# Splitting half of an output projection's weights early, and running dense steps ahead of two phase borders, in a hybrid recurrence and attention kernel

## The chip, the cores and the metric

The kernel runs on one core of one Trainium2 chip. The metric is device time in microseconds for one execution. Three executions of the kernel before took 2696.61, 2696.66 and 2698.05 us; the median is 2696.66 us.

## The reference, cut to what matters

One layer (DEPTH = 1) over 2048 tokens of width 1024, all in float32. The input is normalised and modulated, multiplied by one combined projection, and the columns go to two branches: a gated linear recurrence in both directions (HGRN2, 8 heads of 128) and a 2-D neighbourhood attention over a 32 x 64 grid (16 heads of 64). Both results are gated, joined to 2048 columns, and multiplied by one output projection `w_out` of 2048 x 1024.

```python
mod = c_act @ ada_w[l] + ada_b[l]
shift, scale, gate = jnp.split(mod, 3, axis=-1)
h = (_layernorm(x) * (1.0 + scale[:, None, :]) + shift[:, None, :]).astype(x.dtype)
proj = h @ w_in[l]
q_h, i_h, zf_fw, zf_bw, g_h, q_n, k_n, v_n, g_n = jnp.split(proj, split_pts, axis=-1)
y_hg = _hgrn2_branch(q_h, i_h, zf_fw, zf_bw, g_h, lb_fw_all[l], lb_bw_all[l], hg_norm_g[l])
o_na = _neighbourhood_attention(na_heads(q_n), na_heads(k_n), na_heads(v_n), rpb[l])
...
y_na = o_na * jax.nn.silu(g_n)
y = jnp.concatenate([y_hg, y_na], axis=-1) @ w_out[l]
z = DEEPNORM_ALPHA * x + gate[:, None, :] * y
x = (_layernorm(z) * ln_g[l] + ln_b[l]).astype(x.dtype)
```

## The kernel before, in words

**Products in three passes.** A float32 product is made of three TensorE passes in the format fp32r. Each operand is split into `hi` (a ScalarE copy into fp32r) and `lo` (a VectorE subtraction of `hi`), and the passes are hi x hi, hi x lo and lo x hi. `proj_mm` (L259) does this for the input projection, `y_mm` (L1418 to L1420) for the output projection. The normalised input lies in SBUF as 32 row tiles `h{g}_{k}_{s}` of 128 x 512: two groups `g` of 512 tokens, eight slices `k` of the width, and `s` for hi and lo. They hold one half of the tokens (1024) at a time.

**Phases.** After the start, phase `n0` does the attention of the first rows; phase `h` does the recurrence, 16 units `i` (8 heads for the first half of the tokens, then 8 for the second); phase `n1` does the rest of the attention, 8 units `u` (a pair of heads each); phase `wo` does the output projection and the last normalisation. The first four token tiles (`NE = 4`) have the first half of their output projection (the eight slices `k` = 0 to 7 of `w_out`, which belong to the recurrence's columns, in two halves `n` of 512 output columns) made already in the last unit of `n1`, by `out_stream`.

**Who sets the order.** On TensorE the order is that of the program (`manual_schedule`). The other queues, SP's DMA queue among them, are ordered by a planner that simulates the program and issues what is ready; `pinned(...)` keeps one instruction behind everything traced before it on its engine. All DMAs here are issued by SP.

**Weaving.** In each unit a generator `mix` (the recurrence's chain `hgrn`, or the attention's `natten_woven`) is interleaved by `weave` with a generator `dense` of projection steps for the next unit. `mix` yields the weight of each of its parts; after each, `dense` is advanced to the same share of its total. A recurrence unit has a sum of 54 and 80 dense steps (10 outputs of 8 steps; the constant `KUS = 0.68` is the planned length of a step); an attention unit a sum of 24 and 48 steps.

**The recurrence's chain** (`hgrn`), for each of two groups `g`: `rates` (L411 to L425), `ends` (L431 to L444), transposes `turned` (L450), the states' updates `updates` (L458), whose PSUM tile is read by `forward_states` (L469, L471) before the second updates can write it, the factors of the scores (L482 to L518), scores (L497, L525), masks (`masked`) and `outputs` (L549, L551).

**Entering n1.** The steps in front of the first unit are written out: keys (`st.k`, copies within SBUF by DMA on L923), queries, a bias table (`st.table`, L702, 480 KB each; three buffers), V tiles (`st.v`, L931), two more tables, and others. Then a stream `vs` of V projections (16 steps, weights split on L250) is advanced by four steps, and the rest of it goes into the first unit's dense work. `scores` (L985, L989) writes PSUM that the softmax (L1002 on VectorE, with the bias table; L1007 on ScalarE) reads.

**Bringing in w_out.** In unit 6 of n1 the dense work runs group by group, so that group 0's row tiles come free in the middle of the unit. From step 7 of 12 on, `wo_load` loads raw slices of `w_out` (L1373, 256 KB each, into buffers `wraw` that the input weights use, too) and `wo_split` splits them into the freed row tiles: ScalarE L1378, pinned, and VectorE L1379. `y_early` loads the recurrence's results (L1384) into `wraw` and `y_split` splits them (L1410 pinned on ScalarE, L1411 on VectorE) at the start of unit 7. The second halves (`n` = 1) are loaded into the buffers `vt` and split in the first steps of unit 7.

Of the kernel before, what the change touches and what calls it, by code (L numbers as in the profile page):

```python
# [10 lines left out]
F32 = mybir.dt.float32  # L11
F32R = mybir.dt.float32r
U32 = mybir.dt.uint32
AF = mybir.ActivationFunctionType
ALU = mybir.AluOpType
# [4 lines left out]
P = 128  # L20
KT = D // P
HALF = 1024
GRP = 512
# [10 lines left out]
WR = 4  # L34
# [3 lines left out]
def body(ctx: ExitStack, tc: tile.TileContext, t):  # L38
    nc = tc.nc
    dve, act, pool, pe = nc.vector, nc.scalar, nc.gpsimd, nc.tensor  # L40
    dma = nc.sync.dma_start
# [5 lines left out]
    hp = main.enter_context(tc.tile_pool(name="hp", bufs=1))  # L47
# [16 lines left out]
    def dram(name, shape, dt=F32):  # L64
        if name in t:
            return t[name]
        return nc.dram_tensor(name, shape, dt, kind="Internal").ap()
# [13 lines left out]
    nb_d = dram("nb_d", (120, 3072))  # L81
    tedge = dram("tedge", (NPAIR, 3, 16, 15, 2, 32))
    tint = dram("tint", (NPAIR, 3, 16, 22, 2, 32))

    cnt = [0]

    def nm(s):
        cnt[0] += 1
        return f"{s}_{cnt[0]}"

    def tl(tag, dt=F32, shape=None):
        if tag in cur["smap"]:
            tag = cur["smap"][tag]
            return sh.tile([P, 512], dt, tag=tag, name=nm(tag), bufs=SH[tag])
        return cur["pool"].tile([P, 512] if shape is None else shape, dt, tag=tag, name=nm(tag), bufs=cur["bufs"].get(tag, 1))
# [31 lines left out]
    def pinned(ins):  # L127
        return tc.keep_in_program_order(ins)
# [176 lines left out]
    def hgrn_init():  # L305
        p = cur["pool"]
        msk["mskd"] = p.tile([P, 3, 32], F32, tag="mskd", name="mskd")
        dma(msk["mskd"], t["mskd"])
        for i in range(2):
            b = p.tile([P, 2 * P], F32, tag=f"pdb{i}", name=f"pdb{i}")  # L310
            pool.memset(b, 0.0)
            pdb.append(b)
        for u in range(NHEAD):
            sfb.append(p.tile([P, P], F32, tag=f"sfb{u}", name=f"sfb{u}"))
# [81 lines left out]

    HTOT = 2 * len(HCOL) * KT * KUS

    def hgrn(u, half, st, tail):

        zs, qs, sgs, vts = st["e"], st["q"], st["sg"], st["v"]
# [139 lines left out]
        def outputs(g, v, pm):  # L541

            po = ps("po")
            for b in range(4):
                sl = slice(b * P, (b + 1) * P)
                bb = g * 4 + b
                has_f = (0, bb) in S
                has_b = not (g == 1 and b == 3)
                pe.matmul(po[:, sl], v[:, sl], pm[:, sl], start=(b == 0), stop=not (has_f or has_b), skip_group_check=True)  # L549
                if has_f:  # L550
                    pe.matmul(po[:, sl], S[0, bb], qibs[0, g][:, sl], start=False, stop=not has_b, skip_group_check=True)  # L551
            os_[g] = po

        for g in range(2):
            v = turned(vts[g], "v")
            next(tail, None)
            cs, ks = {}, {}
            cs[0], ks[0] = rates(0, g)
            yield 5
            next(tail, None)  # L560
            cs[1], ks[1] = rates(1, g)
            de0 = ends(0, g, cs[0], ks[0])
            yield 5
            next(tail, None)
            ke0 = turned(de0, "ke")
            de1 = ends(1, g, cs[1], ks[1])
            kx, qx = diagonal_factors(g, cs, ks)
            yield 3
            next(tail, None)
            forward_states(g, updates(ke0, v))  # L570
            ke1 = turned(de1, "ke")
            yield 3
            next(tail, None)
            pu = updates(ke1, v)
            if g == 0:
                ub = tl("ub")
                act.activation(ub, pu, AF.Copy)
                ubs[g] = ub
            else:
                ubs[g] = pu  # L580
            pb = diagonal(kx, qx)
            lf = [(w, *level_factors(w, g, cs, ks)) for w in (32, 64)]
            yield 6
            next(tail, None)
            pa = ps("pa")
            for w, xk, xq in lf:
                level(w, pa, xk, xq)
            pm = masked(pa, pb)
            yield 5
            outputs(g, v, pm)  # L590
        for _ in tail:
            pass
        return hgrn_tail(u, half, sgs, ubs, decs, qibs, os_, decb_all)
# [708 lines left out]
            except StopIteration as e:  # L1302
                return e.value

    def weave(mix, dense, total, steps, last=0):

        got, done, cum = [], [0.0], 0.0

        def upto(x):
            while done[0] < x and not got:  # L1310
                try:
                    done[0] += next(dense)
                except StopIteration as e:
                    got.append(e.value)

        share = HTOT / total if last else 1.0
        while True:
            try:
                cum += next(mix)
            except StopIteration as e:  # L1320
                tail = e.value
                break
            upto(total * share * cum / steps)
        if last:
            for i, _ in enumerate(tail):
                upto(total * (share + (1 - share) * (i + 1) / last))
        upto(1e9)
        return tail, got[0]
# [14 lines left out]

    with psum_phase("h", *HPS), phase("h", HB, SMH), tc.manual_schedule(engines={mybir.EngineType.PE}):
        hgrn_init()
        tail = iter(())
        for i in range(16):
            half, u = divmod(i, 8)
            if i < 15:
                nxt = hgrn_dense((i + 1) % 8, (i + 1) // 8, i in (6, 7), reload if i == 6 else None)  # L1350
                tail, st = weave(hgrn(u, half, st, tail), nxt, HTOT, HSUM)
            else:
                raws, dense = natten_stream(0, 1)
                st0 = Prep(0, 1, raws)
                for n in ("q", "k0", "k1", "g"):
                    st0.fetch(n)
                weave(hgrn(u, half, st, tail), border_dense(dense), BTOT, HSUM, 9)
# [7 lines left out]
        eng.tensor_tensor(lo, raw, hi, op=ALU.subtract)  # L1365
        wo[k, n] = (hi, lo)

    wraws = {}

    def wo_load(n, *ks):  # L1370
        for k in ks:
            wraws[k, n] = wp.tile([P, 512], F32, tag="wraw", name=nm("wr"), bufs=WR) if n == 0 else tl("wr")
            dma(wraws[k, n], t["w_out"][k * P:(k + 1) * P, n * 512:(n + 1) * 512])  # L1373

    def wo_split(n, *ks):
        for k in ks:
            hi, lo = (hp.tile([P, GRP], F32R, tag=f"h{n}_{k}_{s}", name=nm("wo")) for s in range(2))
            tc.keep_in_program_order(act.activation(hi, wraws[k, n], AF.Copy))  # L1378
            dve.tensor_tensor(lo, wraws[k, n], hi, op=ALU.subtract)  # L1379
            wo[k, n] = (hi, lo)  # L1380

    def y_raw(tt, q):
        raw = wp.tile([P, 512], F32, tag="wraw", name=nm("yr"), bufs=WR)
# [99 lines left out]
    with psum_phase("n1", *NPS), phase("n1", NB1, SM1), tc.manual_schedule(engines={mybir.EngineType.PE}):  # L1483
        natten_init(6, 1)
        st = st0
        for f, *a in ((st.k, 0), (st.k, 1), (st.k, 2), (st.q, 1), (st.table, "mid", 0), (st.v, 0), (st.v, 1), (st.v, 2), (st.v, 3), (st.table, "mid", 1), (st.table, "mid", 3), (st.q, 2), (st.v, 4), (st.gate, 1)):
            f(*a)
        vs = vstream(2, 3)
        for _ in range(4):
            next(vs)  # L1490
        pipe = []
        cts = [(c + u * P) // P for u in range(1, 8) for _ in range(2 if u == 7 else 1) for n, c in NCOL]
        feed = Feed(cts)
        feed.at = 0
        for u in range(8):
            nxt, extra = None, None
            if u < 7:
                raws, dense = natten_stream(u + 1, 1, feed, u + 1 == 7)
                total = NLEN
                if u == 0:  # L1500
                    dense, total = chain(vs, dense), NLEN + 1.5 * VLEN
                nxt = Prep(u + 1, 1, raws)
                if u == 6:
                    extra = {7: [(wo_load, 0, 0, 1)], 8: [(wo_load, 0, 2, 3), (wo_split, 0, 0, 1)], 9: [(wo_load, 0, 4, 5), (wo_split, 0, 2, 3)],
                             10: [(wo_load, 0, 6, 7), (wo_split, 0, 4, 5), (y_early, 0)], 11: [(wo_split, 0, 6, 7), (y_early, 1), (wo_load, 1, 0, 1)]}
            else:
                y_split(0, 1)
                dense, total = out_stream(list(range(NE))), NE * 16 * KUS
                extra = {0: [(wo_split, 1, 0, 1), (wo_load, 1, 2, 3, 4, 5)], 1: [(wo_split, 1, 2, 3), (wo_load, 1, 6, 7)], 2: [(wo_split, 1, 4, 5, 6, 7)]}
            weave(natten_woven(st, nxt, pipe, extra), dense, total, 24)  # L1510
            st = nxt
        sums(pipe, 2)
        turn(pipe, 2)
        turn(pipe, 1)
        sums(pipe, 0)
# [70 lines left out]
```

## Time and profile before

| What | Value |
|---|---|
| Median of three executions | 2696.66 us |
| Profiled execution: time, span | 2697.29 us, 2695.5 us |
| Mean granted TensorE clock | 0.985 |
| TensorE busy | 2591.2 us, 96% |
| VectorE, ScalarE, GpSimd busy | 66%, 53%, 4% |
| DMA moved | 296.45 MB, mean 110 GB/s |
| Phase h, by TensorE's rows | from about 555 to 1765 us |
| Phase n1's scores, by L985 | 1779 to 2365 us |

A row of the timeline has the start in us, the duration in us, the engine, the line, the operation, the tile written and those read, a count, and in brackets the idle time before it with what ended it. A row of the waits has the waiting engine, tile and line, what it waited for, and the sum, the number and the longest in us. A row of the windows has, for a stretch of the span, the busy time of each engine with its number of instructions, then the mean granted clock of TensorE, the busy share of the 16 DMA engines and GB/s. A row of one line's instructions has the shortest, median and longest duration in ns. SPq is the DMA queue of SP.

### The profile page before, as it was taken

The numbers are of one execution on the slowest core, as the hardware profiler recorded it, in microseconds if no ns is written. First come the engines' busy times: TensorE is split into PE (matmuls) and PEld (weight loads), VectorE is DVE, ScalarE is ACT, GpSimd is POOL, SyncE is SP. The second block draws the span as 40 slices with busy tenths as digits, with TensorE's granted clock in tenths as the row PEclk, the third lists the DMA queues.
The fourth block names the chain that finished last, engine by engine and source line by source line (L and its number), as shares of the span: only waits on it lengthen the run. The fifth ranks groups of instructions, "written<-read, shape, count | busy, mean of one in ns | idle before, by whom it ended". The sixth has DMA issues, their size and how long they took to land.

```text
span 2695.5 us, 45977 instructions
## 1 busy us (share of the span) xinstructions
PE 2591.2 (96%) x17328; PEld 2158.9 (80%) x17328; DVE 1766.1 (66%) x4351; ACT 1424.3 (53%) x2808; POOL 106.0 (4%) x143
## 2 busy tenths in 40 slices
PE   4999999989999999999999999989999998899998
PEld 3888888878888888888888888878777776688887
DVE  5445445477777778877777877455777777548443
ACT  4534444366666666666666666444666666431110
POOL 0000000000000000000000000000000000032221
PEclk8999999999999999999999999989999999999999
DMA  6566454212111126212221122354444445444331
GB/s 237 157 189 162 127 165 154 104 52 75 63 63 57 63 75 221 83 38 75 75 79 59 67 68 83 98 161 121 120 134 135 133 128 137 112 147 135 98 94 55
DMA packets 226559, 296.45 MB, mean 110 GB/s; under 512 B 28456, under 2 KB 117288, under 8 KB 226217
## 3 DMA queue, kind: packets, MB, share of 16 engines
q1 hardware_dynamic: 226337, 293.52, 35.4%
q8 instruction: 136, 2.23, 0.3%
q14 instruction: 86, 0.70, 0.1%
HBM read 218.24 MB, written 66.99 MB: 106 GB/s over the span
## 4 chain that ended last, share of the span: by engine, by line
PE 70%; DVE 3%; ACT 2%; DMA 2%; SPq 1%; issue 1%; DVEq 0%; ACTq 0%
PE pj L259 38%; PE ps L1418 4%; PE ps L1420 4%; PE ps L1419 4%; PE ps L1034 3%; PE ps L1053 2%; PE pj L272 2%; PE ps L458 2%; PE ps L450 1%; PE ps L985 1%; PE ps L525 1%; PE ps L497 1%; PE ps L549 1%; PE ps L551 1%; PE ps L989 1%; PE ps L623 1%
## 5 line engine op out<-in xcount | busy, mean ns | idle before, releaser
L259 PE MATMUL pj<-h,wh 128*128 128x512 f32 x4016 | 1284.0, 401 | 10.3 <-ACT h L224 6.2
L259 PEld LDWEIGHTS pj<-h,wh 128*128 128x128 f32 x4016 | 730.7, 189 | 168.6 <-issue 14.5
L259 PE MATMUL pj<-h,wl 128*128 128x512 f32 x2008 | 787.8, 392 | 1.3 <-DVE wl L759 1.3
L259 PEld LDWEIGHTS pj<-h,wl 128*128 128x128 f32 x2008 | 378.0, 188 | 84.7 <-DVE wl L759 1.7
L1007 ACT ACTIVATE pbuf<-pbuf,mx 128x480 f32<-128x480 f32 (+2 forms) x224 | 143.1, 639 | 123.2 <-DVE mx L1002 121.9
L272 PE MATMUL pj<-wh,h 128*128 128x256 f32 x1024 | 196.4, 289 | 0.3 <-ACT e L732 0.3
L1002 DVE CUSTOM_DVE_ANT_1 pbuf<-ps,bias 128x480 f32<-128x480 f32 (+2 forms) x224 | 125.6, 590 | 105.2 <-PE ps L989 79.8
L272 PEld LDWEIGHTS pj<-wh,h 128*128 128x128 f32 x1024 | 164.7, 195 | 4.3 <-issue 2.9
L250 DVE TENSOR_TENSOR wl<-wr,wh 128x512 fp32r<-128x512 f32 x192 | 131.7, 686 | 48.7 <-ACT wh L249 47.7
L249 ACT ACTIVATE wh<-wr 128x512 fp32r<-128x512 f32 x192 | 120.2, 626 | 80.7 <-PE pj L259 69.5
L1040 ACT ACTIVATE pt<-ps 128x512 f32<-128x512 f32 (+1 forms) x128 | 69.0, 539 | 151.0 <-PE ps L1034 150.8
L272 PE MATMUL pj<-wl,h 128*128 128x256 f32 x512 | 146.3, 286 | 0.0
L1038 DVE COPY pt<-ps 128x512 f32<-128x512 f32 (+1 forms) x128 | 79.3, 620 | 86.8 <-PE ps L1034 86.0
L444 DVE TENSOR_TENSOR de<-e,de 128x512 f32<-128x512 f32 x64 | 44.3, 692 | 118.8 <-ACT de L443 117.6
L1034 PE MATMUL ps<-ident,pbuf 128*128 128x128 f32 x776 | 107.0, 275 | 9.5 <-DVE mx L1002 9.5
L1034 PEld LDWEIGHTS ps<-ident,pbuf 128*128 128x128 f32 x776 | 93.3, 142 | 25.7 <-DVE mx L1002 9.9
L1394 ACT ACTIVATE yh<-yr 128x512 fp32r<-128x512 f32 x52 | 32.7, 628 | 134.4 <-PE ps L1419 116.1
L1053 PE MATMUL ps<-pt,V 128*64 128x128 f32 x1408 | 100.8, 279 | 0.2 <-DMA V<-nv 0.2
L1467 DVE TENSOR_TENSOR vt<-ps,gt 128x512 f32<-128x512 f32 x24 | 16.5, 692 | 128.6 <-PE ps L1420 128.6
L272 PEld LDWEIGHTS pj<-wl,h 128*128 128x128 f32 x512 | 99.7, 195 | 0.7 <-issue 0.5
L732 ACT ACTIVATE e<-pj 128x512 f32<-128x512 f32 x100 | 59.3, 594 | 76.4 <-PE pj L259 72.1
L1012 DVE TENSOR_SCALAR pbuf<-pbuf,mx 128x480 f32<-128x480 f32 (+2 forms) x224 | 95.9, 436 | 5.4
(273 smaller groups left out, 4725.2 us busy)
## 6 DMA issues: line engine op xcount, KB each, us to landing
wr<-in_w_in SPq DMA_DIRECT2D x276, 256.0 KB
V<-nv SPq DMA_DIRECT2D x256, 64.0 KB
yr<-yq SPq DMA_DIRECT2D x64, 256.0 KB
bias<-tint SPq DMA_DIRECT2D x24, 480.0 KB
x<-in_x SPq DMA_DIRECT2D x32, 256.0 KB
ada<-in_ada_w SPq DMA_DIRECT2D x16, 512.0 KB
wr<-in_w_v SPq DMA_DIRECT2D x32, 256.0 KB
nv<-vt SPq DMA_DIRECT2D x32, 256.0 KB
```

What stands on the lines that cost most here:

```text
L249: act.activation(hi, raw, AF.Copy)
L250: dve.tensor_tensor(lo, raw, hi, op=ALU.subtract)
L259: pe.matmul(pz, a, b, start=(k == 0 and n == 0), stop=(k == KT - 1 and n == 2))
L272: pe.matmul(pzs[tp][:, i * 256:(i + 1) * 256], a, b, start=(k == 0 and n == 0 and i == 0), stop=(k == KT - 1 and n == 2), skip_group_check ...
L1002: return dve.tensor_tensor_reduce(s[:, 0:nk].rearrange("p (r c) -> p r c", c=32), sc[:, 0:nk].rearrange("p (r c) -> p r c", c=32), bt[:, 0 ...
L1007: act.activation(s[:, 0:nk], s[:, 0:nk], AF.Exp, scale=-1.0, bias=mx[:, 0:1], accum_out=mx[:, 1:2])
L1012: dve.tensor_scalar(s[:, 0:nk], s[:, 0:nk], mx[:, 2:3], 1.0, op0=ALU.mult, op1=ALU.mult)
L1034: pe.transpose(ptp[:, c * P:(c + 1) * P], s[:, c * P:(c + 1) * P], ident)
L1053: pe.matmul(self.po[R][hs_, j * P:(j + 1) * P], self.st.V[c0 + c][:, j * P + hh * 64:j * P + hh * 64 + 64], pts[hh][:, c * P:(c + 1) * P], ...
L1418: pe.matmul(pz, yh[:, kk], wh, start=first, stop=False)
L1419: pe.matmul(pz, yh[:, kk], wl, start=False, stop=False)
L1420: pe.matmul(pz, yl[:, kk], wh, start=False, stop=last)
```

## The change

Three things are changed. The first eight slices of `w_out` (16 tiles of 128 x 512) are loaded and split during the recurrence by `wo_prepare`, one tile after each group's `outputs`, through the buffers `bk`, and both parts are written to DRAM (`wo_d`). In n1 `wo_get` loads both parts from there into the freed row tiles, with no split; it begins at step 6 of unit 6, and the second halves follow at steps 0 to 3 of unit 7. `weave` takes a `lead`: 20 steps of dense work run ahead of the first recurrence unit. In front of n1's first unit the two other bias tables stand ahead of the V tiles, and eight steps of `vs` run in place of four.

```diff
@@ hgrn and before it @@
+    aside = []
+
+    def wo_prepare():
+        for i in range(16):
+            k, n = divmod(i, 2)
+            raw = tl("bk")
+            pinned(dma(raw, t["w_out"][k * P:(k + 1) * P, n * 512:(n + 1) * 512]))
+            yield
+            hi, lo = tl("bk", F32R), tl("bk", F32R)
+            pinned(act.activation(hi, raw, AF.Copy))
+            pinned(dve.tensor_tensor(lo, raw, hi, op=ALU.subtract))
+            for s, z in enumerate((hi, lo)):
+                pinned(dma(wo_d[i][s], z.bitcast(F32)))
...
             outputs(g, v, pm)
+            next(aside[0], None)
@@ weave @@
-    def weave(mix, dense, total, steps, last=0):
+    def weave(mix, dense, total, steps, last=0, lead=0.0):
...
+        upto(lead)
...
-            upto(total * share * cum / steps)
+            upto(lead + (total * share - lead) * cum / steps)
@@ phase h @@
+        aside.append(wo_prepare())
...
-                tail, st = weave(hgrn(u, half, st, tail), nxt, HTOT, HSUM)
+                tail, st = weave(hgrn(u, half, st, tail), nxt, HTOT, HSUM, lead=20 * KUS if i == 0 else 0.0)
@@ w_out in n1: wo_load and wo_split are replaced @@
+    def wo_get(n, *ks):
         for k in ks:
+            wo[k, n] = [hp.tile([P, GRP], F32R, tag=f"h{n}_{k}_{s}", name=nm("wo")) for s in range(2)]
+            for s in range(2):
+                pinned(dma(wo[k, n][s].bitcast(F32), wo_d[2 * k + n][s]))
@@ phase n1 @@
-        for f, *a in ((st.k, 0), (st.k, 1), (st.k, 2), (st.q, 1), (st.table, "mid", 0), (st.v, 0), (st.v, 1), (st.v, 2), (st.v, 3), (st.table, "mid", 1), (st.table, "mid", 3), (st.q, 2), (st.v, 4), (st.gate, 1)):
+        for f, *a in ((st.k, 0), (st.k, 1), (st.k, 2), (st.q, 1), (st.table, "mid", 0), (st.table, "mid", 1), (st.table, "mid", 3), (st.v, 0), (st.v, 1), (st.v, 2), (st.v, 3), (st.q, 2), (st.v, 4), (st.gate, 1)):
...
-        for _ in range(4):
+        for _ in range(8):
             next(vs)
...
-                    dense, total = chain(vs, dense), NLEN + 1.5 * VLEN
+                    dense, total = chain(vs, dense), NLEN + VLEN
...
-                    extra = {7: [(wo_load, 0, 0, 1)], 8: [(wo_load, 0, 2, 3), (wo_split, 0, 0, 1)], 9: [(wo_load, 0, 4, 5), (wo_split, 0, 2, 3)],
-                             10: [(wo_load, 0, 6, 7), (wo_split, 0, 4, 5), (y_early, 0)], 11: [(wo_split, 0, 6, 7), (y_early, 1), (wo_load, 1, 0, 1)]}
+                    extra = {6: [(wo_get, 0, 0, 1)], 7: [(wo_get, 0, 2)], 8: [(wo_get, 0, 3)], 9: [(wo_get, 0, 4, 5)], 10: [(y_early, 0), (wo_get, 0, 6)], 11: [(y_early, 1), (wo_get, 0, 7)]}
...
-                extra = {0: [(wo_split, 1, 0, 1), (wo_load, 1, 2, 3, 4, 5)], 1: [(wo_split, 1, 2, 3), (wo_load, 1, 6, 7)], 2: [(wo_split, 1, 4, 5, 6, 7)]}
+                extra = {i: [(wo_get, 1, 2 * i, 2 * i + 1)] for i in range(4)}
```

More of the change, by code (lines that the diff above doesn't have):

```diff
@@ L83, in body @@
     tint = dram("tint", (NPAIR, 3, 16, 22, 2, 32))
+    wo_d = [dram(f"wod{i}", (2, P, 512)) for i in range(16)]
     cnt = [0]
@@ L1366, in load_wo @@
         wo[k, n] = (hi, lo)
-    wraws = {}
-    def wo_load(n, *ks):
+    def wo_get(n, *ks):
         for k in ks:
[L1372 to L1380, printed above, removed]
+            wo[k, n] = [hp.tile([P, GRP], F32R, tag=f"h{n}_{k}_{s}", name=nm("wo")) for s in range(2)]
+            for s in range(2):
+                pinned(dma(wo[k, n][s].bitcast(F32), wo_d[2 * k + n][s]))
     def y_raw(tt, q):
```

## The prediction

> **What bounds the kernel now.** I read the page's totals first, then the waits of TensorE, then the windows around the long ones.
>
> ```profile
> span 2695.5 us, 45977 instructions
> PE 2591.2 (96%) x17328; PEld 2158.9 (80%) x17328; DVE 1766.1 (66%) x4351; ACT 1424.3 (53%) x2808; POOL 106.0 (4%) x143
> ```
>
> TensorE (PE) is busy 96% of the span and its order is the program's order, so the time is its work plus its holes. The holes, by what ended them (sum, count, longest):
>
> ```profile
> PE pj L1418 <- ACT yh L1410: 9.7, 2, 8.5
> PE ps L1034 <- DVE mx L1002: 9.5, 1, 9.5
> PE ps L458 <- DVE Sf L469: 8.2, 1, 8.2
> PE ps L985 <- DVE mx L1002: 6.2, 1, 6.2
> PE ps L985 <- DMA KA<-KA: 3.3, 1, 3.3
> ```
>
> Single long waits lie at three borders: 8.2 us at the recurrence's entry (the row L458), 3.3 and 6.2 us at its exit, 9.5 and 8.5 us where w_out's first half is brought in. Smaller ones beside them:
>
> ```profile
> 566.17 0.30 PE L450 MATMUL ps<-ident,de 128*128 128x128 f32 x1 [0.35 <-DVE de L444]
> 571.03 0.38 PE L458 MATMUL ps<-v,ke 128*128 128x128 f32 x1 [0.82 <-ACT ke L452]
> 2288.59 0.49 PE L985 MATMUL ps<-KB,Q 128*128 128x480 f32 x1 [2.13 <-DVE pt L1038]
> 2348.60 0.50 PE L1418 MATMUL pj<-wo,yh 128*128 128x512 f32 x1 [1.21 <-ACT yh L1410]
> ```
>
> A hole costs more than its length. These windows begin where each long wait ends; PEclk is the granted clock:
>
> ```profile
> core 0: us, PE busy (x) PEld busy (x) DVE busy (x) ACT busy (x) POOL busy (x), PEclk, DMA share, GB/s
> 583.80:590.00 6.20, 6.20 (x80) 5.39 (x81) 2.96 (x7) 3.22 (x5) 0.00 (x0) 0.56 0.01 3
> 1779.20:1786.00 6.80, 6.78 (x37) 5.74 (x38) 3.20 (x9) 1.96 (x5) 0.00 (x0) 0.75 0.43 136
> 1800.90:1810.00 9.10, 9.10 (x46) 7.80 (x47) 6.86 (x19) 4.67 (x11) 0.00 (x0) 0.62 0.69 190
> 2271.80:2277.00 5.20, 5.16 (x22) 4.34 (x22) 3.42 (x9) 3.90 (x10) 0.00 (x0) 0.66 0.23 80
> 2288.60:2292.00 3.40, 3.40 (x23) 2.57 (x25) 1.58 (x5) 0.00 (x0) 0.00 (x0) 0.56 0.89 192
> 2301.20:2307.00 5.80, 5.74 (x18) 4.62 (x19) 2.74 (x7) 3.65 (x10) 0.00 (x0) 0.58 0.90 262
> ```
>
> PE's busy time times (1 - PEclk) is the time lost to the low clock: 2.7, 1.7, 3.5, 1.8, 1.5 and 2.4 us. Holes and clock together: entry 0.35 + 0.82 + 8.2 + 2.7 = 12.1 us; exit 3.3 + 1.7 + 6.2 + 3.5 = 14.7; w_out 9.5 + 1.8 + 2.1 + 1.5 + 8.5 + 2.4 + 1.2 = 27.0. That is 53.8 us, the most that the change can win.
>
> [...]
>
> **Part 1, entry: 20 dense steps ahead (`lead`).** Nothing is added; 20 of the 80 projection steps of the first unit's partner run before its chain. The price of a step and the state of the other engines in the hole:
>
> ```profile
> 598.43 0.62 PE L259 MATMUL pj<-h,wh 128*128 128x512 f32 x2
> 599.11 0.62 PE L259 MATMUL pj<-h,wh 128*128 128x512 f32 x2
> ```
> ```profile
> 577.00:581.00 4.00, 0.00 (x0) 0.00 (x0) 4.00 (x12) 3.67 (x9) 0.00 (x0) 0.75 0.22 66
> 581.00:585.00 4.00, 1.21 (x6) 1.24 (x7) 3.85 (x10) 1.47 (x3) 0.00 (x0) 0.50 0.00 0
> ```
>
> Steps start 0.68 us apart. The wait at L458 stands after 16 of the chain's 54 parts: 80 x 16/54 = 23.7 steps preceded it, now 20 + 60 x 16/54 = 37.8 do, 14.1 more or 9.6 us, against 9.4 us of holes. What moves with the steps: 14.1 of them are 1.8 outputs of 8 steps, so about two weight splits (0.69 us of DVE each, by the split rows of part 2) and two ACT copies go into a stretch where VectorE and ScalarE are full until about 584 us, and the loads of those weights come earlier on SP, which the DMA share of 0.22 and 0.00 leaves free. DVE's backlog, which the wait at L458 hangs on, thus ends some 1.4 us later, and the part behind has 9.6 us less cover. Between 0 (the chain moves with it) and 12.1 I take 9.5: the cover is as long as the holes, less 1.4 of backlog and about as much of clock.
>
> **Part 2, exit: two bias tables ahead of the V loads, four more steps of the V projection ahead of the scores.**
>
> ```profile
> 1789.16 0.69 DVE L250 TENSOR_TENSOR wl<-wr,wh 128x512 fp32r<-128x512 f32 x1 [2.19 <-ACT wh L249]
> 1792.04 0.69 DVE L250 TENSOR_TENSOR wl<-wr,wh 128x512 fp32r<-128x512 f32 x1 [2.19 <-ACT wh L249]
> 1800.09 0.66 DVE L1002 CUSTOM_DVE_ANT_1 pbuf<-ps,bias 128x480 f32<-128x480 f32 x1 [7.35 <-DMA bias<-tint]
> ```
> ```profile
> 1768.99 0.59 SPq L702 DMA_DIRECT2D bias<-tint  x1
> 1791.39 0.58 SPq L702 DMA_DIRECT2D bias<-tint  x1
> ```
>
> V steps follow each other in 2.88 us (two weight splits), so four are 11.5 us, more than the 9.5 us of the two holes. The 6.2 us hole is the second bias table: issued at 1791.39, 22.4 us behind the first, it landed as the DVE wait of 7.35 ended at 1800.09. Issued behind the first it would land well before the scores, now at about 1787.5. The cost: two tables (480 KB each) go past the V loads and, on SP, perhaps past the KA/KB copies for which the 3.3 us wait stood, delaying those by two issues (1.2 us) and the two transfers (about 3 us at the rate below), still inside 11.5. The V loads are needed only at the first sums. The four steps bring their splits, evictions and stores along, between splits behind which DVE idled 2.19 us each. The unit that loses the cover had 12 V steps in it and keeps 8. Between 0 and 14.7 I take 11.5.
>
> **Part 3, w_out.** What it removes is ScalarE waiting in order for DMAs, with the softmax's exponentials queued behind:
>
> ```profile
> 2262.89 0.63 ACT L1378 ACTIVATE wo<-wr 128x512 fp32r<-128x512 f32 x1 [7.62 <-DMA wr<-in_w_out]
> 2269.95 0.63 ACT L1378 ACTIVATE wo<-wr 128x512 fp32r<-128x512 f32 x1 [3.69 <-DMA wr<-in_w_out]
> 2295.01 0.63 ACT L1378 ACTIVATE wo<-wr 128x512 fp32r<-128x512 f32 x1 [6.99 <-DMA wr<-in_w_out]
> 2300.58 0.63 ACT L1410 ACTIVATE yh<-yr 128x512 fp32r<-128x512 f32 x1 [4.42 <-DMA yr<-yq]
> 2303.88 0.63 ACT L1410 ACTIVATE yh<-yr 128x512 fp32r<-128x512 f32 x1 [2.15 <-DMA yr<-yq]
> ```
>
> The three L1378 rows go; their 18.3 us of waiting lie under the 9.5 us and most of the 8.5 us hole. The two L1410 rows stay: `y_split` still waits for y, whose loads now find their buffers free of w_out.
>
> What it adds there: 32 loads of 256 KB for 16, pinned in SP's order. A load waits for a row tile that PE frees. It is traced behind 15/24 of the dense steps and the tile's last use is behind 12/24, so 6 steps (4.1 us) lie between; were it late, V loads, KA/KB copies, bias tables and y, all on SP, would wait behind it. The second halves are pinned behind the last KB copy and used from the 17th to the 24th step of `out_stream`. Late next is the DMA:
>
> ```profile
> 1055.00:1075.00 20.00, 20.00 (x108) 17.20 (x108) 16.28 (x45) 13.13 (x26) 0.10 (x1) 1.00 0.89 310
> 2254.00:2310.00 56.00, 35.85 (x217) 28.33 (x216) 31.73 (x84) 26.46 (x60) 0.00 (x0) 0.79 0.62 156
> 2291.00:2295.00 4.00, 1.76 (x20) 1.51 (x16) 0.00 (x0) 0.00 (x0) 0.00 (x0) 0.82 1.10 182
> 2303.00:2307.00 4.00, 4.00 (x15) 3.22 (x15) 2.05 (x6) 3.12 (x8) 0.00 (x0) 0.61 0.91 260
> ```
>
> At 1055 the same kind of transfer (row tiles reloaded) ran at 310 GB/s for a share of 0.89, so 256 KB takes 0.75 us of all engines. The stage used 0.62 x 56 = 34.7 us; twelve raw loads in it go (-9) and 32 come (+24): 49.7 us. The second halves are first used up in `out_stream`'s steps to the 24th:
>
> ```profile
> 2328.49 0.50 PE L1418 MATMUL pj<-wo,yh 128*128 128x512 f32 x1
> ```
>
> By the count of such starts this is the 23rd or 24th step, so the stage to its end lasted 2328.5 - 2254 = 74 us and lasts 74 - 27 = 47 without holes. At the share of 0.91 that lasts in the fourth row, 49.7 needs 55 us: 8 us too long, and 2 us of clock with it. So of 27.0 I take 17; the ends are 27 (it fits) and 5 (rival B).
>
> [...]
>
> **Part 4, w_out prepared in the recurrence.** Sixteen times a load, an ACT copy (0.63 us, above), a DVE subtraction and two stores, all pinned, spread over the 16 group ends of the recurrence's first half (the last split over the first of the second).
>
> ```profile
> L1379 DVE TENSOR_TENSOR wo<-wr,wo x8: 671/690/693, 2263.5 to 2295.7; 128x512 fp32r<-128x512 f32 x8
> ```
> ```profile
> 642.30:1161.00 518.70, 518.70 (x3940) 439.43 (x3939) 391.00 (x1003) 333.27 (x619) 0.69 (x7) 1.00 0.26 89
> 1222.00:1675.00 453.00, 449.82 (x3348) 376.42 (x3348) 353.65 (x820) 299.11 (x555) 0.23 (x1) 1.00 0.21 72
> ```
>
> 16 x 0.69 = 11 us take DVE from 391/518.7 = 0.75 to 0.78, the load of the second half (353.65/453), where PE idles 3.2 us in 453. So up to 3.6 us, cover as now nothing; a gain is excluded, since nothing PE waits for gets earlier. I take 1. 48 transfers of 0.75 us are 36 us of DMA in a stretch with a share of 0.26. A store waits on SP for the split, and weight loads queue behind it: rival D.
>
> **Sum.** 9.5 + 11.5 + 17 - 1 = 37. The profiled execution took 2697.29 us (1.8 around its span), the median 2696.66, 0.6 less: 2697.3 - 37 = 2660.3, or 2660 against the median.
>
> **Rivals.**
> B: the DMA queue is the new wait in full: w_out's tiles and y come as late as ScalarE waited before. The border wins 5 in place of 17: 2672. For it: share 0.90 at 2301 already, and the pins. Against: y and w_out no longer wait for each other's buffers.
> C: the two leads only shift the waits (DVE full to 584; SP puts the tables where it had them). Parts 1 and 2 bring 3 together: 2678.
> D, slower: the pinned stores hold SP until DVE has split, and the next column's weights come late, at each of 16 calls. It decides from 38/16 = 2.4 us a call; a hole of 2 us with 1.5 of clock is 56 us: 2660 - 1 + 56 = 2715. Against: no PE idle in 518.7 us, and half 2's higher DVE load costs little.
> E: replanned order elsewhere eats the gain, or the pins hold back SP by as much: within 5.4 us of 2697.
>
> **How the numbers follow.** Forecast 0.57 (2648 to 2670 by itself), B 0.22, C 0.08, D 0.08, E 0.05. 0.2% is 5.4 us, about what a measurement of this kernel can tell from no change. Forecast, B and C are faster: 0.87; E same: 0.05; D slower: 0.08. The range runs from 2647 (50 of the 53.8 us) to 2683 (C with a poorer w_out border), leaving out D, E and the tails.
>
> **What would show it.** Right: no L458 wait above 2 us and a clock of 1.00 near 585; the second bias issued within 3 us of the first; no ACT wait on w_out, the L1410 wait under 4 us; PE idle near 1 us or less between 640 and 1160. Wrong: PE waiting for a w_out tile by DMA for over 10 us, KA/KB copies landing after 1790, holes of 2 us in the recurrence.

## The result, and the profile after

The kernel after takes 2687.0 us (median of four, 2683.22 to 2687.9) against 2697.36 (2696.61 to 2698.6) on the same chip: 10.4 us faster, a ratio of 0.9957 with a 95% interval of 0.9944 to 0.997. 2660 was predicted, and the time lies outside the predicted range of 2647 to 2683. The profiled execution took 2687.64 us. (In the profile of after, numbers of lines behind L400 are 9 to 18 higher than before: y's split, L1410, is now L1420. e2 and e3 have nearly the numbers of before; the other experiments are shifted by up to 8 more.)

The page's totals, then the waits of TensorE (sum, count, longest), in the kernel after:

```profile
span 2685.8 us, 46076 instructions
PE 2585.7 (96%) x17328; PEld 2154.1 (80%) x17328; DVE 1764.1 (66%) x4351; ACT 1423.0 (53%) x2808; POOL 106.6 (4%) x143
...
PE pj L273 <- ACT vt L279: 12.8, 2, 11.9
PE ps L1050 <- ACT pt L1056: 12.2, 2, 11.2
...
PE ps L473 <- DVE Sf L484: 4.0, 2, 2.8
PE pj L1428 <- DMA wo<-wod: 3.6, 1, 3.6
PE pj L260 <- ACT wh L774: 2.9, 1, 2.9
```

The long waits of before are gone from this list: the one for the bias table's softmax at the exit, the one for it at w_out, and the 8.5 us for `yh`. The entry's 8.2 is now 2.8. But two waits stand here that before had not: 11.9 us for an eviction (the copy of a result out of PSUM) of the V projection (L279) at the exit and 11.2 us for an eviction of transposed tiles (L1056) at the w_out border. Both evictions are ScalarE's and short (1.07 us for two at 1808.10, 0.47 us for one at 2279.98); it came to them late. Its timeline at the exit, with the idle time in front and what ended it in brackets:

```profile
1805.78 0.63 ACT L953 ACTIVATE sg<-bk 128x512 f32<-128x512 f32 x1 [18.24 <-DMA bk<-ng]
1806.91 0.63 ACT L319 ACTIVATE sg<-sg 128x512 f32<-128x512 f32 x1 [0.49 <-DVE sg L318]
1807.57 0.63 ACT L320 ACTIVATE sg<-sg 128x512 f32<-128x512 f32 x1
1808.10 1.07 ACT L279 ACTIVATE vt<-pj 128x512 f32<-128x512 f32 x2
```

ScalarE stood 18.24 us at L953, the exponential of the gate of n1's unit 1, which nothing needs while unit 0 runs; the eviction that TensorE waited for was three instructions behind it. Before, the same gate ran at 1813.47 with its data there. SP's queue shows why its load came late; then SP and ScalarE at w_out:

```profile
1778.27 7.48 SPq L947 DMA_DIRECT2D V<-nv  x8
...
1801.93 0.32 SPq L910 DMA_DIRECT2D bk<-ng  x1
```
```profile
2260.93 8.85 SPq L1390 DMA_DIRECT2D wo<-wod  x6
2269.87 3.76 SPq L1394 DMA_DIRECT2D yr<-yq  x2
```
```profile
2277.73 0.63 ACT L1420 ACTIVATE yh<-yr 128x512 fp32r<-128x512 f32 x1 [12.81 <-DMA yr<-yq]
2278.27 0.60 ACT L1023 ACTIVATE pbuf<-pbuf,mx 128x384 f32<-128x384 f32 x1
```

The first split of y stood 12.81 us for its load, and behind it the last exponentials of unit 6's softmax. So the change removed ScalarE's waits on w_out, and the planner put another waiting operation in front of the same work. It could, although y's split is `pinned`: these exponentials are traced before the split and ran behind it, so the pin does not tie an instruction to all earlier ones, as the description of the kernel before has it. That it ties it to the one traced just before it is the likely reading; no run tests it.

Two windows of after, at the w_out border:

```profile
2270.00:2280.00 10.00, 0.00 (x0) 0.00 (x0) 1.18 (x4) 2.27 (x7) 0.00 (x0) 0.62 0.93 281
2280.00:2290.00 10.00, 9.49 (x54) 7.27 (x55) 8.36 (x25) 6.91 (x17) 0.00 (x0) 0.70 0.46 148
```

TensorE does nothing for 10 us while the DMA engines are busy at a share of 0.93. So two theories stand. **Theory 1 (order):** the holes are operations that wait for a load and stand in their engine's order ahead of urgent work, as in the rows of 18.24 and 12.81 us; order them behind and the holes go. **Theory 2 (bytes):** at w_out the loads themselves are too many (32 of 256 KB for 16), and any order only moves the wait.

### The profile page after: what moved, and what is told of

Same layout as the page of the kernel before. It is cut to its first block, busy times and chain, and to the rows that moved or that the text cites. A ratio compares the mean times of both kernels' runs of the same rounds, so it can differ in the third digit from the quotient of the medians.

```text
span 2685.8 us, 46076 instructions
## 1 busy us (share of the span) xinstructions
PE 2585.7 (96%) x17328; PEld 2154.1 (80%) x17328; DVE 1764.1 (66%) x4351; ACT 1423.0 (53%) x2808; POOL 106.6 (4%) x143
## 4 chain that ended last, share of the span: by engine, by line
PE 67%; DMA 4%; DVE 4%; ACT 2%; issue 1%; SPq 1%; DVEq 0%; ACTq 0%
PE pj L260 37%; PE ps L1430 4%; PE ps L1428 4%; PE ps L1429 4%; PE ps L1069 2%; PE ps L1050 2%; PE ps L473 2%; PE pj L273 2%; PE ps L465 1%; PE ps L1001 1%; PE ps L540 1%; PE ps L564 1%; PE ps L566 1%; PE ps L512 1%; DMA bias<-tint 1%; PE ps L1005 1%
## 5 line engine op out<-in xcount | busy, mean ns | idle before, releaser
L1056 ACT ACTIVATE pt<-ps 128x512 f32<-128x512 f32 (+1 forms) x128 | 69.1, 540 | 148.1 <-PE ps L1050 147.9
L1477 DVE TENSOR_TENSOR vt<-ps,gt 128x512 f32<-128x512 f32 x24 | 16.5, 692 | 128.5 <-PE ps L1430 128.5
```

## The experiments

| run | median us | before, same chip | ratio, 95% interval |
|---|---|---|---|
| e1 gate pinned | 2679.4 | 2695.86 | 0.9935, 0.9922 to 0.9947 |
| e2 exit alone | 2698.78 | 2695.86 | 1.0007, 0.9998 to 1.0016 |
| e3 lead alone | 2689.65 | 2695.86 | 0.9978, 0.9968 to 0.9988 |
| e4 preparation alone | 2696.56 | 2695.86 | 0.9996, 0.9987 to 1.0004 |
| e5 w_out alone | 2689.63 | 2695.97 | 0.9977, 0.9968 to 0.9986 |
| e6 y first | 2689.3 | 2695.97 | 0.9975, 0.9966 to 0.9985 |
| e7 gate, y first | 2685.6 | 2695.97 | 0.9962, 0.9949 to 0.9976 |
| e8 gate, key, y first | 2675.39 | 2695.97 | 0.9931, 0.9918 to 0.9944 |
| e9 gate, key | 2672.98 | 2696.1 | 0.9909, 0.9892 to 0.9925 |
| e10 + y behind softmax | 2672.89 | 2696.1 | 0.9913, 0.9898 to 0.9927 |
| e11 + y products later | 2667.07 | 2696.1 | 0.9891, 0.9876 to 0.9906 |
| e12 e10, half the bytes | 2667.82 | 2696.1 | 0.9895, 0.988 to 0.991 |
| e13 e11, y low on GpSimd | 2664.33 | 2695.8 | 0.9884, 0.9868 to 0.9901 |
| e14 e13, half the bytes | 2661.06 | 2695.8 | 0.9871, 0.9856 to 0.9886 |

### The four parts, each alone on the kernel before

**e2, the exit.**

```diff
-(st.table, "mid", 0), (st.v, 0), ... (st.v, 3), (st.table, "mid", 1), (st.table, "mid", 3), ...
+(st.table, "mid", 0), (st.table, "mid", 1), (st.table, "mid", 3), (st.v, 0), ... (st.v, 3), ...
-        for _ in range(4):
+        for _ in range(8):
-    dense, total = chain(vs, dense), NLEN + 1.5 * VLEN
+    dense, total = chain(vs, dense), NLEN + VLEN
```

> The kernel before with the edits at the recurrence's exit alone (two bias tables ahead of the V loads, eight V steps ahead of the scores). The traces of the two kernels put this part at 2 us worse than before (time lead of 6.6 us at 1757, 4.5 us at 1948). Theory 1: the gate is issued as early as in the changed kernel, a hole of 10 to 12 us stands at 1800, time 2697.4 + 2 = 2699 (2696 to 2702). Rival (the new hole needs the other parts, for example the earlier w_out traffic): both old holes of 3.3 and 6.2 us are gone with nothing in their place, time 2683 to 2687.

2698.78: nothing won, by its interval 0.5 us faster to 4.3 slower. The timelines of ScalarE and of TensorE in this run:

```profile
1813.87 0.63 ACT L937 ACTIVATE sg<-bk 128x512 f32<-128x512 f32 x1 [17.39 <-DMA bk<-ng]
```
```profile
1816.82 0.58 PE L272 MATMUL pj<-wh,h 128*128 128x256 f32 x1 [11.03 <-ACT vt L278]
1840.51 1.22 PE L259 MATMUL pj<-h,wh 128*128 128x512 f32 x2 [2.94 <-ACT wh L758]
```

This part alone brings the gate's stand and the new hole; the old holes of 3.3 and 6.2 us have gone, as foreseen, and 11.0 came.

**e3, the entry** (`weave`'s `lead` of 20 steps, nothing else).

> The kernel before with the 20 dense steps ahead of the recurrence alone. In the changed kernel the end of unit 0 came 6.3 us earlier, and only 4.3 us were left at 1672. Theory (the lead is good for 6.3, and the w_out preparation costs the 2.0): the L458 hole is 2 to 3 us, the lead is still 6 us at 1672, time 2691 (2689 to 2692). Rival (the thinner dense work after the lead costs the 2 us by itself, as in the hole of 1.23 us at 1075): 4.3 us left at 1672, time 2693 (2692 to 2695).

2689.65: 6.2 us won, as the first theory had it. At the same row sum in the recurrence's last part (L330, 1676.57 before) this run's trace stands at 1668.39, 8.2 earlier. That trace is of the fastest of nine executions, 2683.32 us, so it shows where the time goes and not how much of it a typical execution wins.

**e4, the preparation** (`wo_prepare` and its call after each group; w_out is still loaded and split as before).

> The kernel before with the preparation of w_out in the recurrence alone: 16 loads, splits and double stores to DRAM that nothing reads; w_out is still brought in as before. Theory (this costs the 2 us lost between 640 and 1672): time 2699 (2698 to 2702), with small holes between 600 and 1200. Rival (it is covered): 2697.4 within 1 us. Against my rival D of the prediction (2.4 us or more a call, 38 us): at most 4 us are expected.

2696.56: no difference that the interval shows (3.5 us faster to 1.1 slower). A window of the recurrence, its columns as before:

```profile
642.30:1161.00 518.70, 518.70 (x3939) 439.44 (x3940) 397.50 (x1017) 340.34 (x635) 0.69 (x7) 1.00 0.33 112
```

TensorE has no idle time in it, VectorE has 6.5 us more to do than the 391.00 of before, and the DMA share goes from 0.26 to 0.33. The pinned stores hold TensorE up nowhere in this window. With the lead it is not quite free: the trace of after has a wait of 1.23 us at the states' updates (L473, 1075.09) that neither e3's nor e4's has.

**e5, w_out** (preparation and `wo_get`, without the entry and the exit).

> The kernel before with the w_out part alone: preparation in the row units, direct loads of the split halves, the mid tables and the leads as before. Theory 1 (in the changed kernel ScalarE reaches y's split, which waits for y, ahead of unit 6's last softmax): the waits of before at this border go, an 11 us hole behind y and some 3 us behind a w_out half come, so about 5 us gain, 2691. Theory 2 (the border is bound by the bytes of the loads, whatever the order): 2690 to 2693, the same. The prediction's term for this part, 17 us: 2679.

2689.63: 6.3 us won. Both theories had foreseen about that; the 17 us of the prediction are excluded. Its two holes at this border, as in after:

```profile
2280.38 0.90 PE L1050 MATMUL ps<-ident,pbuf 128*128 128x128 f32 x3 [11.77 <-ACT pt L1056]
2312.22 0.79 PE L1428 MATMUL pj<-wo,yh 128*128 128x512 f32 x1 [3.34 <-DMA wo<-wod]
```

The three parts sum to 6.2 - 2.9 + 6.3 = 9.6 us, against 10.4 for the whole.

### Order at the exit

**e1, the gate kept in program order** on the kernel after:

```diff
-            act.activation(sg, raw, AF.Exp, scale=-1.0)
+            e = act.activation(sg, raw, AF.Exp, scale=-1.0)
+            if self.half and self.p == 1 and R == 1:
+                pinned(e)
```

> The changed kernel with one ScalarE instruction tied down: the first activation of the gate of unit 1 (the L953 row that stood 18.24 us for its DMA) may no longer be issued ahead of what is traced before it. Theory 1 (order: ScalarE stands in its order behind an instruction that nobody needs yet, and the V projection's PSUM eviction waits behind it): the 11.9 us hole of TensorE at 1808 goes, with the 0.95 us beside it perhaps and 3 us of low clock; time 2687 - 13 = 2674 (2670 to 2678). Rival (DMA: the V loads and bias tables fill the queue, and whatever comes next is late): the hole stays as a wait for another DMA, time 2684 to 2688.

2679.4: 16.5 us under before, where after has 10.4, and 1.4 us short of the range expected. The 11.88 us hole is gone; the next operation behind a load shows up, on ScalarE and then on TensorE:

```profile
1802.89 0.63 ACT L938 ACTIVATE KA<-bk 64x512 fp32r<-64x512 f32 x1 [8.20 <-DMA bk<-nk]
```
```profile
1807.80 1.97 PE L1052 MATMUL ps<-ident,pbuf 128*128 128x128 f32 x8 [5.46 <-DVE pt L1056]
```

It is unit 1's first key piece, fetched beside the gate behind the same V loads.

**e9, this key piece kept in program order, too** (the same three lines around L938).

> The changed kernel with unit 1's gate and first key piece kept in program order, y's loads where the change has them. The 5.5 us hole that the pinned gate left at the exit goes (the gate alone: 2679.4), and the y loads moved ahead cost some 6 us in the two runs that had them: 2671 to 2674. Rival: the 10 us between the runs with and without the pinned key piece came from y's place as well: 2678 or more.

2672.98: 23.1 us under before, 6.6 more than e1. At the exit only these waits of over 0.6 us are left:

```profile
1771.57 0.39 PE L273 MATMUL pj<-wh,h 128*128 128x256 f32 x1 [0.94 <-ACT vt L279]
1818.98 0.73 PE L260 MATMUL pj<-h,wh 128*128 128x512 f32 x2 [2.93 <-ACT wh L774]
```

Two pins bring 23.1 - 10.4 = 12.7 us. If the parts add, the exit is worth these less the 2.9 that it had lost alone (e2): 9.8, near the 11.5 predicted for it. Theory 1 holds here.

### Order and bytes at w_out

**e6, e7, e8: y's loads ahead of w_out's**, alone, with the gate, and with gate and key piece.

```diff
-  8: [(wo_get, 0, 3)], 9: [(wo_get, 0, 4, 5)], 10: [(y_early, 0), (wo_get, 0, 6)], 11: [(y_early, 1), (wo_get, 0, 7)]
+  8: [(y_early, 0, 1), (wo_get, 0, 3)], 9: [(wo_get, 0, 4, 5)], 10: [(wo_get, 0, 6)], 11: [(wo_get, 0, 7)]
```

> The changed kernel with y's four loads issued at step 8, ahead of w_out's fourth half-row and all later ones, instead of at steps 10 and 11 behind twelve of them. Theory 1 (order): the 11.2 us hole before the transposes of unit 6 shrinks to under 3 us, 2679 against 2687. Theory 2 (bytes): the hole stays or comes back as a wait of the same length for a w_out half in front of the first w_out products; 2685 to 2688.

> The pinned gate and y's loads ahead, together. Theory 1: the two gains add, 7 to 8 us each: 2671. Theory 2: only the gate's is left, 2679.

> As the run before, and unit 1's first key piece, whose conversion stood 8.2 us in ScalarE's order for its load with the gate pinned, is kept in program order too. Theory 1: the 5.5 us hole that was left at the exit goes with it: 2666, or some 5 us under the run with gate and y. Rival: the softmaxes are late for another reason (scores, the bias tables), or another operation behind a load takes the place: within 1.5 us of that run.

6.7, 10.4 and 20.6 us under before, each less than without y's move (10.4, 16.5 and 23.1), though only e7's interval lies clear of that of its partner. The gain that order foresaw did not come. The edit had missed its aim: in e6 the planner moved the split earlier, too, and the load still took until 2269:

```profile
2269.18 0.63 ACT L1420 ACTIVATE yh<-yr 128x512 fp32r<-128x512 f32 x1 [15.43 <-DMA yr<-yq]
```

So these three say that moving y's loads alone does not help, and nothing on the two theories at this border. The difference of e8 and e7, 10.2 us, again shows the key piece.

**e10, y's first splits held behind unit 6's last exponentials** (on e9; `lastp` is the last of them):

```diff
-                tc.keep_in_program_order(act.activation(hi, yraws[tt, q], AF.Copy))
+                with tc.issue_after(lastp[0].ins):
+                    tc.keep_in_program_order(act.activation(hi, yraws[tt, q], AF.Copy))
```

> As the run before, with y's first four splits held on ScalarE behind unit 6's last softmax exponentials. Order (theory 1): the 11 us hole before the transposes of unit 6 goes, but TensorE's next products take y, which lands some 3 us before that hole ended; 3 to 5 us faster than the run before. Bytes (theory 2): the wait moves whole to y's products or to a w_out half; within 1.5 us of the run before.

2672.89: the same as e9, as theory 2 had said. But the trace shows order once more; ScalarE, then TensorE:

```profile
2262.92 0.63 ACT L1428 ACTIVATE yh<-yr 128x512 fp32r<-128x512 f32 x1 [8.06 <-DMA yr<-yq]
```
```profile
2267.22 0.77 PE L1006 MATMUL ps<-KB,Q 128*128 128x480 f32 x1 [10.97 <-ACT pt L1063]
```

The exponentials are out; the eviction of their transposed tile (0.47 us), for which the next scores waited these 10.97 us, is now what stands behind y: it ran at 2266.70, behind y's third split.

**e11, y's splits behind that eviction, too, and TensorE's y products three parts later** in unit 7 (`lastp` taken at L1061):

```diff
-                y_split(0, 1)
+                extra[0] = [(y_split, 0, 1)] + extra[0]
-            weave(natten_woven(st, nxt, pipe, extra), dense, total, 24)
+            weave(natten_woven(st, nxt, pipe, extra), dense, total, 24, lead=0.0 if u < 7 else -10 * KUS)
```

> As the run before the last, with y's splits held on ScalarE behind unit 6's last transposed tile and TensorE's y products started three of 24 steps later in unit 7. Order (theory 1): TensorE has unit 6's and 7's own work while y lands; the hole shrinks to under 4 us, 6 to 9 us faster than with gate and key pinned alone. Bytes (theory 2): TensorE catches up with the loads, and the waits for w_out halves grow by what the hole loses; within 2 us of it.

2667.07: 5.9 us faster than e9, just under the 6 to 9 of theory 1. ScalarE's first wait for y is 0.85 us. The hole that was to shrink to under 4 us has instead moved behind VectorE:

```profile
2273.40 0.80 PE L1438 MATMUL pj<-wo,yl 128*128 128x512 f32 x1 [9.28 <-DVE yl L1429]
```
```profile
2270.43 0.66 DVE L1023 CUSTOM_DVE_ANT_1 pbuf<-ps,bias 128x480 f32<-128x480 f32 x1 [9.45 <-DMA bias<-tint]
...
2272.66 2.48 DVE L1429 TENSOR_TENSOR yl<-yr,yh 128x512 fp32r<-128x512 f32 x4
```

VectorE stood for unit 7's bias table, and y's low halves were behind it.

**e13, those four subtractions on GpSimd.**

```diff
-                dve.tensor_tensor(lo, yraws[tt, q], hi, op=ALU.subtract)
+                (pool if tt < 2 else dve).tensor_tensor(lo, yraws[tt, q], hi, op=ALU.subtract)
```

> As the run with the y products later, with the four subtractions for y's first low halves on GpSimd, which has nothing to do there, and not on VectorE, which stood 9.45 us for unit 7's bias table ahead of them. Order: TensorE's 9.3 us wait for y's low half falls to under 3 us, and the next wait is the bias table's own (its softmaxes are on TensorE's way some 6 us later); 3 to 7 us faster than 2667. Bytes: the wait stays a wait for y or a w_out half; within 1.5 us of 2667.

2664.33: 2.7 us faster than e11, a little less than foreseen, and 31.5 under before, the best of the kernels that compute the whole result. VectorE and TensorE:

```profile
2268.66 0.66 DVE L1023 CUSTOM_DVE_ANT_1 pbuf<-ps,bias 128x480 f32<-128x480 f32 x1 [9.79 <-DMA bias<-tint]
```
```profile
2269.39 0.77 PE L1006 MATMUL ps<-KA,Q 128*128 128x480 f32 x1 [4.00 <-DVE mx L1023]
```

VectorE stands as long as before, but only 4.0 us of it reach TensorE.

**e12 and e14, half of the loads** and so of the bytes of w_out's first eight row tiles, on e10 and on e13. They leave out the low halves, so they only measure:

```diff
-    wo[k, n] = [hp.tile(...) for s in range(2)]
-    for s in range(2):
+    wo[k, n] = [hp.tile(...) for s in range(2 if n else 1)] * (1 if n else 2)
+    for s in range(2 if n else 1):
```

> As the run with y behind the softmax, with the low halves of w_out's first eight row tiles not loaded (the high ones are used twice, so the output is not the reference's): 2 MB less to move at this border, the order of ScalarE the same. Bytes (theory 2): y lands earlier and the waits at this border fall by 6 to 10 us against the run with the same order. Order alone (theory 1): 0 to 2 us.

> As the run before, without the low halves of w_out's first eight row tiles (the high ones used twice, so the output is not the reference's). Order: the table of unit 7 lands earlier too, but TensorE has y's work meanwhile: 0 to 2 us faster than the run before. Bytes: what is left of the waits there goes, 4 to 7 us faster.

2667.82, 5.1 us faster than e10 with the order alike, and 2661.06, 3.3 faster than e13. ScalarE's stand for y and TensorE's hole in e12, to be set against 8.06 and 10.97:

```profile
2260.18 0.63 ACT L1428 ACTIVATE yh<-yr 128x512 fp32r<-128x512 f32 x1 [4.97 <-DMA yr<-yq]
```
```profile
2264.05 0.77 PE L1006 MATMUL ps<-KB,Q 128*128 128x480 f32 x1 [7.43 <-ACT pt L1063]
```

Both runs lie between what the two theories foresaw (0 to 2 us and 6 to 10 in e12, 0 to 2 and 4 to 7 in e14). So the loads are a cause as well: they decide how late y comes, the order decides how much of the lateness TensorE sees. Order, from e9 to e13 and with the four subtractions' move counted in, is worth 2672.98 - 2664.33 = 8.7 us; with it mended, halving the loads brings 3.3 us in place of 5.1. Both theories hold at w_out, and order is the larger.

How e14 wins its 3.3 us is less clear. Its wait behind the bias table is as long as in e13 (4.00):

```profile
2267.88 0.77 PE L1006 MATMUL ps<-KA,Q 128*128 128x480 f32 x1 [4.25 <-DVE mx L1023]
```

In its trace TensorE's waits of over 0.35 us in the 13 us before it sum to 1.8 us against 3.0 in e13's, and y's first products (L1436 to L1438, 128x512, about 2262 to 2264) started 0.23 us apart against 0.43. Nor is it w_out alone that y's loads stand behind. SP's own waits (sum, count, longest), in after around the w_out border:

```profile
SPq L1390 <- DMA bias<-tint: 4.9, 1, 4.9
SPq L1394 <- DMA bias<-tint: 2.5, 1, 2.5
```

By the profile, SP stood 4.9 us among w_out's loads and 2.5 us at y's until a bias table had landed, and in e11 5.5 and 2.9. What a bias table costs there, whether moving unit 7's ahead of w_out's loads would take the last 4.0 us, and whether it is the bytes or the number of loads that counts, was not tried.

## Why the prediction was wrong

**Entry, 9.5 predicted, 6.2 measured.** The mechanism was right, only the size was off. The term that was too large is "the cover is as long as the holes": the L458 wait fell from 8.15 to 2.79 us (under 2 was foreseen), and another of 1.38 us came behind it at 628, since the later part has less cover. With 1.5 us of low clock behind the first (below) 5.7 of the 12.1 us stay in after's trace, and it had won 6.3 by the end of the first unit. In e3's trace the clock's loss had gone, and 8.2 were won. Of after's 6.3 only 4.3 were left at 1672; 1.2 of the 2.0 lost are the wait at 1075, the rest was not found.

**Exit, 11.5 predicted, between 0.5 won and 4.3 lost.** What was foreseen of the tables came: two are issued together at 1762.42 and the third 7.6 us later, and no softmax waits for them. The step that failed is "The four steps bring their splits, evictions and stores along", which looked at VectorE's idle time and took ScalarE's for granted. The evictions stand in ScalarE's order, and I didn't ask what else stands there: gate and key piece of unit 1, whose loads SP has behind the V loads. With both held back, e9 gets the part's worth.

**w_out, 17 predicted, 6.3 measured with its preparation.** The rows that were to go went, 18.3 us of ScalarE's waits. The step that failed is "The two L1410 rows stay: `y_split` still waits for y, whose loads now find their buffers free of w_out". A free buffer was not what y's load waited for next: twelve halves of w_out stood ahead of it, and ScalarE came to it 12.81 us early (under 4 us was foreseen) with unit 6's softmax behind. Rival B, 5 us for this border, had nearly the size. Its mechanism, the DMA queue in full, was a part of it: halving w_out's loads brings 3.3 to 5.1 us, mending the order 8.7.

**Preparation, 1 predicted.** e4's interval holds both 1 us and nothing. TensorE has no idle time in its window, so the cover named for it hides it; rival D, 56 us, is refuted.

**Sum.** 37 predicted, 10.4 measured, and 31.5 in e13, with two pins, y's splits and products later, and four subtractions on another engine. The holes had been read rightly; whether they closed hung on the planner's order as well as on the change. Rival C's 3 us for entry and exit together is also near what e2 and e3 give, 6.2 - 2.9 = 3.3, but by luck: the tables did move and the entry was won. B and C had been weighed as alternatives, and the time came out about where both prices hold at once (2660 + 12 + 18 = 2690).

## What to carry to other kernels

Where a planner sets the order, and an engine stands at an operation until its load lands (ScalarE 18.24 us at L953, with the eviction that TensorE waited for three instructions behind it), a removed wait is not a removed hole (in e2 holes of 3.3 and 6.2 us went and one of 11.0 came): list every operation near it that waits for a load, and what the engine would do behind each if the planner set it first. Look in the trace after a change for a long idle in front of an operation that nothing needs yet, and hold that one back by an edge to the urgent work. Moving its load ahead was no substitute here: in e6 the planner answered the earlier load with an earlier wait (15.43 us to 2269). A pin need not hold an instruction behind all that was traced before it; look in the trace at what it was set behind.

## What was unexpected of the hardware

The granted clock after a hole does not follow from the hole's length alone. After a wait of 2.79 us in the kernel after and of 2.78 us in e3, at the same place, the windows are (after first, then e3; the clock is the third number from the end):

```profile
586.40:590.00 3.60, 3.51 (x73) 3.28 (x74) 0.01 (x1) 0.60 (x1) 0.00 (x0) 0.56 0.02 5
```
```profile
586.40:590.00 3.60, 3.60 (x80) 3.10 (x80) 1.88 (x5) 0.99 (x2) 0.00 (x0) 1.00 0.02 5
```

0.56 and 1.00: 3.51 x 0.44 = 1.5 us lost in one and none in the other. Behind before's hole of 8.15 us the clock was 0.56, too (the first of the prediction's six windows). What decided between 0.56 and 1.00 was not shown.

ScalarE took nothing else while it stood 18.24 us in front of L953 in the kernel after, though TensorE waited 11.88 us, to 1808.74, for an eviction three instructions behind it.
